# A DoRA forward kernel: block 5 loaded in halves, the resumption moved to the third chunk of block 2, a group of stores moved by two chunks

## The chip, the cores and the metric

One NeuronCore of a Trainium2 chip runs the kernel; the other cores are idle. The metric is the time of one execution on the device in microseconds (us), lower is better. Each kernel was run several times beside the kernel before on the same chip; "faster" and "slower" need more than 2%.

## The reference

```python
W_adapted = W + scale * (lora_A @ lora_B)                       # 256 x 256, rank 16
W_norm    = np.sqrt(np.sum(W_adapted ** 2, axis=0, keepdims=True) + 1e-8)
W_final   = W_adapted / W_norm * m
y = x.reshape(-1, 256) @ W_final                                # x: 16 x 2048 x 256, fp32
```

The weights are small. x has 32768 rows of 1 KB, 33.6 MB, and y is as large: the kernel is a copy through the core with a small matrix product on the way.

## The kernel before

x is cut into 8 blocks of 4096 rows (4 MB), each of 8 chunks of 512 rows; two chunks are a pair, the unit of work. Five block buffers stand in SBUF, and y is written back into the buffer of its x. Blocks 5, 6 and 7 therefore have to wait until blocks 0, 1 and 2 are stored. Loads are issued from SyncE, stores from ScalarE; GpSimd casts a pair to bf16, TensorE transposes it, VectorE copies the transposes to SBUF, TensorE multiplies, ScalarE copies the product back into the x buffer.

```python
loads += [((XBUFS - 1) * CH, CH - 3)]
loads += [(XBUFS * CH - 3 + c, 1) for c in range(3)] + units[XBUFS:]       # (first chunk, chunks)
...
F = NBLK - XBUFS          # 3
G = F * CH                # chunk 24
stores = [(b * CH, CH, 19 + b) for b in range(F - 1)]                      # (first chunk, chunks, issued after chunk)
stores += [(G - CH, CH // 2, 24), (G - CH // 2, CH // 2, 24)]              # stores 2 and 3: block 2
FIRST = len(stores)
stores += [(G + c, 1, G + 3) for c in range(4)]                            # four stores of one chunk
stores += [(G + 4, CH - 4, 47)]                                            # the group: chunks 28-31,
stores += [(b * CH, CH, max(47, (b + 1) * CH - 1)) for b in range(F + 1, NBLK - 1)]  # 32-39, 40-47
stores += [(g0, cnt, g0 + cnt - 1) for g0, cnt in units[-2:]]
HALF = FIRST - 2          # store 2
...
for n in range(len(loads)):                    # SyncE
    if loads[n][0] == XBUFS * CH - 3:
        nc.sync.wait_ge(sem("store0"), 16)
    if loads[n][0] == XBUFS * CH:              # block 5 and all behind it
        for k in range(HALF + 1):
            nc.sync.wait_ge(sem(f"store{k}"), 16)
    if loads[n] == units[-1]:
        nc.sync.wait_ge(sem(f"store{HALF + 1}"), 16)
    load_x(n)
...
for p in range(NPR):                           # GpSimd, one pair at a time
    ...                                        # wait for the load of the pair's chunks
    if p == REST:                              # 15: compute rests until store 2 has landed
        nc.gpsimd.wait_ge(sem(f"store{HALF}"), 16)
    ...                                        # cast
...
with nc.Fori(0, NPR // 2, 1, engines=[PE], head_slot={PE: 128}):   # TensorE
    turned(1)      # transposes of the next pair come before
    product(0)     # the product of this one
    turned(0)
    product(1)
```

Of the kernel before, what the change touches and what calls it, by code (L numbers as in the profile page):

```python
# [11 lines left out]
def kernel(  # L12
# [26 lines left out]
    NBLK = N // BLK  # L39
# [3 lines left out]
    XBUFS = 5  # L43
    CH = DJ // J
# [57 lines left out]
    units = [(b * CH, CH) for b in range(NBLK - 1)]  # L102
    units += [(NCH - CH, CH // 2), (NCH - CH // 2, CH // 2)]
    loads = [(0, 2), (2, 2), (4, CH - 4)] + units[1 : XBUFS - 1]


    loads += [((XBUFS - 1) * CH, CH - 3)]
    loads += [(XBUFS * CH - 3 + c, 1) for c in range(3)] + units[XBUFS:]
    load_of = {g: n for n, (g0, cnt) in enumerate(loads) for g in range(g0, g0 + cnt)}


# [2 lines left out]
    F = NBLK - XBUFS  # L114
    G = F * CH
    stores = [(b * CH, CH, 19 + b) for b in range(F - 1)]
    stores += [(G - CH, CH // 2, 24), (G - CH // 2, CH // 2, 24)]
    FIRST = len(stores)
    stores += [(G + c, 1, G + 3) for c in range(4)]
    stores += [(G + 4, CH - 4, 47)]  # L120
    stores += [(b * CH, CH, max(47, (b + 1) * CH - 1)) for b in range(F + 1, NBLK - 1)]
    stores += [(g0, cnt, g0 + cnt - 1) for g0, cnt in units[-2:]]
    HALF = FIRST - 2

# [4 lines left out]
    def sem(name):  # L129
        if name not in sems:  # L130
            sems[name] = tc.alloc_semaphore(name)
        return sems[name]
# [10 lines left out]
    def load_x(n):  # L143
        nc.sync.dma_start(
            out=in_sbuf(*loads[n]), in_=in_dram(x_flat, *loads[n])
        ).then_inc(sem(f"load{n}"), 16)
# [15 lines left out]
    for n in range(len(loads)):  # L162
        if loads[n][0] == XBUFS * CH - 3:
            nc.sync.wait_ge(sem("store0"), 16)
        if loads[n][0] == XBUFS * CH:


            for k in range(HALF + 1):
                nc.sync.wait_ge(sem(f"store{k}"), 16)
        if loads[n] == units[-1]:  # L170
            nc.sync.wait_ge(sem(f"store{HALF + 1}"), 16)
        load_x(n)

# [12 lines left out]
    for p in range(NPR):  # L186
        b, c = divmod(p, PRB)
# [66 lines left out]
    for g in range(NCH):  # L254
        b, c = divmod(g, CH)
# [123 lines left out]
```

## Time and profile before

| | kernel before |
|---|---|
| time, median of the first 3 runs | 162.56 us (162.53 to 162.67) |
| span of the profiled run | 161.3 us |
| moved | 67.42 MB, mean 418 GB/s |
| both DMA queues' share of the span | 98.1% |
| busiest compute engine | TensorE, 61% |
| last loads end, by packet records | 115.6 to 116.2 us |
| first packets of the group of stores | 115.6 to 116.2 us |

In the profile lines PE is TensorE (PEq its sequencer), POOL GpSimd, DVE VectorE, ACT ScalarE (ACTq issues the stores) and SP SyncE. PEclk is the granted share of TensorE's clock: "warm" below means 1.00, "cold" 0.50. q1 is the queue of the loads, q10 that of the stores; both run on the same 16 DMA engines. A packet's record has its start, duration, size and queue. A DMA share above 1 in a stretch comes from packets that overlap on an engine. The lines on which this reading rests are in the prediction.

### The profile page before, as it was taken

How to read it: one execution, taken by the hardware profiler on the slowest of the kernel's cores; microseconds unless marked ns; L12 is line 12 of the kernel's file. 1: busy time of each engine (PE TensorE's matmuls, PEld its weight loads, DVE VectorE, ACT ScalarE, POOL GpSimd, SP SyncE). 2: the span in 40 equal slices, each digit the busy share in tenths (PEclk: the TensorE clock that was granted, in tenths of full speed). 3: DMA queues.
4: the chain of work that ended last, by engine and by line, in shares of the span. 5: the costliest groups of instructions: out<-in, count | busy, mean ns of one | idle time of the engine just before them, and what ended most of it. 6: DMA issues, size and time to landing. Idle time of an engine off the chain costs nothing. (4 is left out here: it accounts for less than half of the span.)

```text
span 161.3 us, 2012 instructions
## 1 busy us (share of the span) xinstructions
PE 98.1 (61%) x786; PEld 85.6 (53%) x786; DVE 46.6 (29%) x44; ACT 64.1 (40%) x67; POOL 62.9 (39%) x39
## 2 busy tenths in 40 slices
PE   0490899999997920000799949999999980000000
PEld 0260789999996710000689937999799970000000
DVE  0539533535443500000224413445344500000000
ACT  3010068686776370000057643686767681000000
POOL 1174327868684000002938066497667400000000
PEclk9999999999999985555569995999999996555555
DMA  5999999999899999899999999999999999999994
GB/s 163 429 453 459 390 512 398 390 512 398 374 487 439 390 463 456 363 419 422 400 434 424 437 455 422 396 453 431 412 487 398 422 479 398 408 496 398 398 439 211
DMA packets 4357, 67.42 MB, mean 418 GB/s; under 512 B 626, under 2 KB 643, under 8 KB 1667
## 3 DMA queue, kind: packets, MB, share of 16 engines
q1 hardware_dynamic: 2160, 33.82, 49.2%
q10 hardware_dynamic: 2194, 33.59, 48.9%
q14 instruction: 3, 0.02, 0.0%
HBM read 33.85 MB, written 33.55 MB: 418 GB/s over the span
## 5 line engine op out<-in xcount | busy, mean ns | idle before, releaser
L258 ACT COPY x_sb<-y_ps 128x1024 f32<-128x1024 f32 x64 | 62.2, 1015 | 61.5 <-PE y_ps L318 60.2
L199 POOL CAST xb<-x_sb 128x2048 bf16<-128x2048 f32 x32 | 60.4, 1895 | 62.8 <-DMA out_dram<-x_sb 24.7
L318 PE MATMUL y_ps<-w_final,xt 128*128 128x256 bf16 x512 | 66.5, 286 | 2.5 <-PEq L293 2.5
L240 DVE COPY xt<-xt_ps 128x1024 f32<-128x1024 f32 x32 | 39.2, 1224 | 74.3 <-PE xt_ps L304 74.3
L318 PEld LDWEIGHTS y_ps<-w_final,xt 128*128 128x128 bf16 x512 | 52.3, 103 | 10.9 <-issue 3.2
L304 PE MATMUL xt_ps<-identity,xb 128*128 128x128 f32 x264 | 37.2, 288 | 25.7 <-PEq L293 25.7
L304 PEld LDWEIGHTS xt_ps<-identity,xb 128*128 128x128 f32 x264 | 32.3, 150 | 27.7 <-issue 27.2
L274 PE MATMUL y_ps<-identity,a_nat 128*16 128x128 f32 x2 | 0.6, 396 | 4.1 <-DMA a_nat<-in_lora_A_dram 4.1
L285 PE MATMUL y_ps<-sq,ones 128*128 128x256 f32 x4 | 2.1, 675 | 1.6 <-DVE sq L225 1.6
L250 ACT ACTIVATE norm<-y_ps,eps_col 128x256 f32<-128x256 f32 x1 | 0.5, 473 | 5.6 <-PE y_ps L285 5.6
L236 DVE TENSOR_TENSOR w_final<-wam,rnorm 128x256 bf16<-128x256 f32 x2 | 2.5, 1266 | 0.0
L285 PEld LDWEIGHTS y_ps<-sq,ones 128*128 128x128 f32 x4 | 1.2, 326 | 2.3 <-DVE sq L225 2.1
L274 PEld LDWEIGHTS y_ps<-identity,a_nat 128*16 128x16 f32 x2 | 0.1, 88 | 4.1 <-issue 4.1
L248 ACT ACT_TABLE_LOAD x1 | 1.3, 1283 | 2.4 <-issue 2.4
L205 POOL MEMSET xb<- 128x2048 bf16 x1 | 1.8, 1804 | 0.7 <-PE xt_ps L304 0.7
L233 DVE RECIPROCAL rnorm<-norm 128x256 f32<-128x256 f32 x1 | 1.7, 1747 | 0.0
L227 DVE COPY m_all<-y_ps 128x256 f32<-128x256 f32 x1 | 0.4, 424 | 3.3 <-PE y_ps L290 3.3
L290 PE MATMUL y_ps<-m_row,ones 1*128 1x256 f32 x2 | 1.2, 710 | 0.0
L216 DVE CAST b_bf<-b_nat 16x256 bf16<-16x256 f32 x1 | 0.3, 280 | 3.2 <-DMA b_nat<-in_lora_B_dram 3.2
L221 DVE SCALAR_TENSOR_TENSOR wa<-y_ps,w_nat 128x512 f32<-128x512 f32 x1 | 0.7, 692 | 0.8 <-PE y_ps L278 0.8
L278 PE MATMUL y_ps<-b_bf,aT 16*128 16x256 bf16 x2 | 0.6, 402 | 0.5 <-DVE aT L218 0.5
L290 PEld LDWEIGHTS y_ps<-m_row,ones 1*128 1x128 f32 x2 | 0.5, 308 | 0.7 <-issue 0.7
(13 smaller groups left out, 3.3 us busy)
## 6 DMA issues: line engine op xcount, KB each, us to landing
x_sb<-in_x_dram SPq DMA_DIRECT2D x5, 4096.0 KB, 28.7
out_dram<-x_sb ACTq DMA_DIRECT2D x5, 4096.0 KB, 20.9
out_dram<-x_sb ACTq DMA_DIRECT2D x5, 2048.0 KB, 26.7
x_sb<-in_x_dram SPq DMA_DIRECT2D x3, 2048.0 KB, 33.4
x_sb<-in_x_dram SPq DMA_DIRECT2D x1, 2560.0 KB, 44.7
x_sb<-in_x_dram SPq DMA_DIRECT2D x2, 1024.0 KB, 6.0
out_dram<-x_sb ACTq DMA_DIRECT2D x4, 512.0 KB, 43.8
x_sb<-in_x_dram SPq DMA_DIRECT2D x3, 512.0 KB, 19.5
```

The source lines that it names most:

```text
L199: nc.gpsimd.tensor_copy(out=xb_bufs[p % NXB][:], in_=x_bufs[b % XBUFS][:, 2 * c * J : 2 * (c + 1) * J, :],).then_inc(sem("rounded"), 1)
L205: nc.gpsimd.memset(xb_bufs[NPR % NXB][:], 0.0).then_inc(sem("rounded"), 1)
L221: nc.vector.scalar_tensor_tensor(out=wa[:], in0=ab_ps, scalar=float(scale), in1=w_nat[:], op0=ALU.mult, op1=ALU.add).then_inc(dv, 1)
L233: nc.vector.reciprocal(out=rnorm[:], in_=norm[:]).then_inc(dv, 1)
L236: i = nc.vector.tensor_mul(out=w_final[:, t], in0=wam[:, t], in1=rnorm[:])
L240: nc.vector.tensor_copy(out=xt_bufs[p % NXT][:].rearrange("p r t -> p (r t)").bitcast(FP32), in_=xt_ps[p % 2][:],).then_inc(sem("copied"), 1)
L248: nc.scalar.activation(out=warm[:], in_=eps_col[:], func=AF.Sqrt)
L258: nc.scalar.copy(out=x_bufs[b % XBUFS][:, c * J : (c + 1) * J, :], in_=y_ps[g % 2][:]).then_inc(sem("room"), 1)
L285: i = nc.tensor.matmul(n2_ps, ones[:], sq[:, t, :], start=(t == 0), stop=(t == KC - 1))
L290: nc.tensor.matmul(mb_ps, ones[0:1, :], m_row[:], start=True, stop=True).then_inc(pe, 1)
L304: i = nc.tensor.transpose(xt_ps[p % 2][:, j * P : (j + 1) * P], xb_bufs[p % NXB][:, j, :].bitcast(FP32), identity[:],)
L318: i = nc.tensor.matmul(y_ps[h][:, j, :], xt_bufs[p % NXT][:, r : r + P, t], w_final[:, t, :], start=(t == 0 and (j % (J // 2)) == 0), stop ...
```

## The change

Its intent is to resume sooner after the rest (GpSimd's wait for store 2 ahead of pair 15): store 2 covers three chunks instead of four, so that the loads and the compute waiting for it are released earlier, and block 5 comes in two halves, so that its first pairs need not wait for the whole block. The group of three stores is moved from chunk 47 to chunk 49. Since store 3 now begins one chunk earlier, with a chunk whose place the first half of block 7 takes, the wait for it is moved one load earlier too.

```diff
--- before.py
+++ after.py
@@ -105,7 +105,9 @@
 
 
     loads += [((XBUFS - 1) * CH, CH - 3)]
-    loads += [(XBUFS * CH - 3 + c, 1) for c in range(3)] + units[XBUFS:]
+    loads += [(XBUFS * CH - 3 + c, 1) for c in range(3)]
+
+    loads += [(XBUFS * CH, 4), (XBUFS * CH + 4, CH - 4)] + units[XBUFS + 1 :]
     load_of = {g: n for n, (g0, cnt) in enumerate(loads) for g in range(g0, g0 + cnt)}
 
 
@@ -114,11 +116,11 @@
     F = NBLK - XBUFS
     G = F * CH
     stores = [(b * CH, CH, 19 + b) for b in range(F - 1)]
-    stores += [(G - CH, CH // 2, 24), (G - CH // 2, CH // 2, 24)]
+    stores += [(G - CH, 3, 24), (G - CH + 3, CH - 3, 24)]
     FIRST = len(stores)
     stores += [(G + c, 1, G + 3) for c in range(4)]
-    stores += [(G + 4, CH - 4, 47)]
-    stores += [(b * CH, CH, max(47, (b + 1) * CH - 1)) for b in range(F + 1, NBLK - 1)]
+    stores += [(G + 4, CH - 4, 49)]
+    stores += [(b * CH, CH, max(49, (b + 1) * CH - 1)) for b in range(F + 1, NBLK - 1)]
     stores += [(g0, cnt, g0 + cnt - 1) for g0, cnt in units[-2:]]
     HALF = FIRST - 2
 
@@ -167,7 +169,7 @@
 
             for k in range(HALF + 1):
                 nc.sync.wait_ge(sem(f"store{k}"), 16)
-        if loads[n] == units[-1]:
+        if loads[n] == units[-2]:
             nc.sync.wait_ge(sem(f"store{HALF + 1}"), 16)
         load_x(n)
 
```

## The prediction

> **What bounds the kernel now.** I read the page first: the rows of forty slices, the queues, the chain of waits. Lines of the page of the kernel before:
>
> ```profile
> span 161.3 us, 2012 instructions
> ...
> PEclk9999999999999985555569995999999996555555
> DMA  5999999999899999899999999999999999999994
> ...
> q1 hardware_dynamic: 2160, 33.82, 49.2%
> q10 hardware_dynamic: 2194, 33.59, 48.9%
> ...
> PE 10%; ACT 1%; ACTq 1%; issue 0%
> ```
>
> The 16 DMA engines are busy in every slice but the first and the last; loads (q1) and stores (q10) together fill 98.1% of the span. The chain of waits covers only 12% of it: it ends at the issue of the last store, 27 us before the end, since behind that issue lies nothing but a backlog of stores. So only an idle DMA engine can cost time. To see whether any stretch has slack, the view by stretches:
>
> ```profile
> core 0: us, PE busy (x) PEld busy (x) DVE busy (x) ACT busy (x) POOL busy (x), PEclk, DMA share, GB/s
> 4.00:44.00 40.00, 33.64 (x245) 28.39 (x246) 19.62 (x21) 17.85 (x19) 22.74 (x13) 1.00 1.01 435
> ...
> 104.00:113.00 9.00, 9.00 (x85) 8.35 (x83) 4.73 (x4) 6.04 (x7) 6.65 (x4) 1.00 1.03 439
> 113.00:116.00 3.00, 2.71 (x25) 2.23 (x24) 1.39 (x2) 2.05 (x3) 2.20 (x2) 1.00 1.02 429
> 116.00:156.00 40.00, 16.48 (x151) 15.06 (x149) 6.12 (x5) 13.37 (x14) 8.04 (x5) 0.73 1.00 432
> ```
>
> The DMA share (next to last column) is 1.00 or more, also in 113 to 116 us, where the last loads hand over to the last group of stores. 67.42 MB at 432 GB/s take 156.1 us; the other 5.2 us of the span are start, tail and small packets. Order alone cannot win 2% (3.3 us) here; it can lose it.
>
> Last, instructions in order of time around the resumption and the hand-over (start, us, engine, what, idle before it):
>
> ```profile
> 75.73 3.73 POOL L199 CAST xb<-x_sb 128x2048 bf16<-128x2048 f32 x2 [24.69 <-DMA out_dram<-x_sb]
> ...
> 94.03 5.57 POOL L199 CAST xb<-x_sb 128x2048 bf16<-128x2048 f32 x3 [5.21 <-DMA x_sb<-in_x_dram]
> ...
> 96.08 1.11 PE L304 MATMUL xt_ps<-identity,xb 128*128 128x128 f32 x8 [2.32 <-PEq L293]
> ...
> 96.98 3.57 PE L318 MATMUL y_ps<-w_final,xt 128*128 128x256 bf16 x16
> ...
> 104.94 3.73 POOL L199 CAST xb<-x_sb 128x2048 bf16<-128x2048 f32 x2 [1.56 <-DMA x_sb<-in_x_dram]
> ...
> 109.12 1.91 PE L318 MATMUL y_ps<-w_final,xt 128*128 128x256 bf16 x16
> 110.20 1.93 ACT L258 COPY x_sb<-y_ps 128x1024 f32<-128x1024 f32 x2 [0.69 <-PE y_ps L318]
> ...
> 112.23 1.38 ACTq L149 DMA_DIRECT2D out_dram<-x_sb  x3
> ```
>
> GpSimd resumes at 75.73 (chunks 0 to 18 and 19 stored), waits for block 5 until 94.03 and for block 6 until 104.94; chunk 47 is copied out by 112.13, and its store group (10 MB, three DMAs) is issued at 112.23. In the packet records of the trace the loads end at 115.7 to 116.6 and the first packets of that group start at 115.6: no hole, and about 2 us to spare (an issue on an idle ACT queue reached its first packet in 1.5 us at the start of the program: 0.90 to 2.36).
>
> **What the Trainium skill says.** "DMA: Bandwidth & Descriptors", section "Queues, rings and completion order": each DMA engine goes round-robin between the queues that have work, a whole packet at a time. The trace agrees: from 84 to 92 us q1 has 96 packets and q10 95, but 3.15 MB against 0.32. The same page, "Specifications", puts the fabric ceiling at 435 GB/s; the trace holds 432, so the queues are at it. "TensorE: Matmul & The Clock Gate", section "Part 1: The HAM clock gate": after an idle window of some 3.4 us the PE clock is halved, and a busy window restores it; windows run free. The trace agrees and is harsher: the 2.32 us gap before 96.08 was enough, 16 products then took 3.57 instead of 1.91 us, and the granted clock was 0.50 from about 97.0 to 100.4 us.
>
> **The change, part by part.**
>
> Three chunks instead of four. Store 2 has 8 packets an engine; at 432/16 = 27 GB/s a 16 KB packet takes 0.61 us, a 12 KB one 0.46. 8 x 0.15 = 1.2 us earlier resumption: 74.5 instead of 75.73. The bytes only move into the next store (5 chunks), so that both are done as before at about 81; the loads behind the wait queue up behind three small loads on q1 anyway (these run to about 82). Gain in DMA time: none. Compute is 1.2 us earlier, and has slack.
>
> Block 5 in halves. In the packet records block 5's packets begin at 82.3. Each 32 KB load packet (1.21 us) alternates with a 4 KB packet of the four one-chunk stores (0.16): 8 x 1.37 = 11.0 us, which fits 82.3 to 93.2, plus 0.8 for landing = 94.03. In halves the row is 16 KB, so 16 rounds of 0.61 + 0.16 = 12.3 us: the first half is landed at about 82.3 + 6.2 + 0.8 = 89.3, the second at 95.4. So compute on block 5 starts 4.8 us earlier, but 8 more small store packets have been let in, and block 6 lands 8 x 0.16 = 1.3 us later: 106.2 instead of 104.94. The loads' end stays where it was (about 115.9 on the mean engine), as the same bytes have to pass before it.
>
> Compute then. PE needs 2.62 us a pair warm. Pair 20 is cast at 89.3, transposed when PE is free at about 92.5, with no gap; pair 22 is cast 95.4 to 97.3, and the last product PE can do without block 6 (pair 22's, as a product follows the next pair's transposes) ends at about 103.1. Then PE idles until pair 24 is cast: 106.2 + 1.89 = 108.1, a gap of 5.0 us. By what 2.3 us did, the clock falls to half.
>
> Stores at 49 instead of 47. Warm, from the end of pair 24's cast: 0.13 to the transposes, 0.9 to product 23, 2.62 to product 24, 1.08 to the first copy of it, 1.93 for two copies: 6.7 us, so the issue is at 108.1 + 6.7 + 0.1 = 114.9. Cold, the restart at 77.62 (end of the first cast) shows the same steps: its fourth copy ended at 86.99, 9.4 us later, 2.7 more than warm. How long it stays cold depends on where the window falls; I take 1.6 to 3.0 more: issue at 116.5 to 117.9. First packet 1.0 to 1.5 us after that: 117.6 to 119.3. Against loads that end at 115.9 this is a hole of 1.7 to 3.4 us in the DMA queues, the four one-chunk stores being done by then. Nothing fills it later: everything behind it is stores at full rate.
>
> Sum: 162.56 + 0 (earlier resumption) + 0.1 (small packets) + about 2.5 (hole) = 165.1; I put the centre at 164.8 for the cases below.
>
> **The rivals.** (1) PE stays warm, or block 6 lands no later: issue at 114.9 or earlier, first packet at about 116.2, hole 0.3 us or less; time 162.6 to 163.2. For it: the margin between 114.9 and 115.9 is near enough to the start-up time. Against: the clock fell in the smaller gap. (2) The split mends a loss: in 80 to 84 us small packets of both queues meet (by packet records 392 GB/s instead of 432, 0.37 us lost), and a tail; all such losses together are under 1 us: 161.8 to 162.4. For it: PE no longer pauses at 94. Against: that pause cost nothing, as the DMA share was full. (3) The work saved early arrives late at the end: last products later by some 2 to 3 us. Costs nothing: the last store is issued 27 us before the end, over a backlog of 24 us and more. (4) Both the cold phase and the start-up are at their longest, and small packets of the resumed queue add to it: 3.4 us or more, 166 and above.
>
> **Range and chances.** I give the hole of 1.7 to 3.4 us some seven in ten, rivals 1 and 2 together one in four, more than that the rest. Range 162.6 to 166.0. The 2% line lies at 165.8, at the upper end of the hole: slower 0.13, same 0.86, faster 0.01.
>
> **What would show it.** Resumption of GpSimd at about 74.5; casts of block 5 at about 89.3 and 95.4; block 6 at about 106.2; an idle PE of about 5 us before the transposes of pair 24 and a granted clock of 0.50 after it; the issue of three stores after 116; a DMA share well under 1 somewhere in 115 to 119 us; and the same 1.00 in all stretches else. Wrong would be: a group of stores issued before 115 us with a full DMA row (then rival 1), or a time under 162.3 (rival 2: a loss that I took for fixed).

## More of the kernel before

The product of pair p runs after the transposes of pair p + 1. Chunk 47 is in pair 23, so even it needs the cast of pair 24, the first pair of block 6.

## The result

| | before | changed |
|---|---|---|
| median | 162.63 us (162.53 to 163.10, 6 runs) | 164.61 us (163.95 to 165.17, 6 runs) |
| ratio | 1 | 1.0114 (95%: 1.0084 to 1.0144) |
| span of the profiled run | 161.3 us | 163.1 us |

The change costs 1.1%, 2.0 us, which is within 2%. Ratios here are the mean time of one kernel's runs over that of the other's runs of the same rounds, so not quite the ratio of the medians. Executions over 1.5% slower than the fastest of the same kernel are left out of the means.

Lines of the page of the changed kernel, the counterparts of those that the prediction shows:

```profile
span 163.1 us, 2014 instructions
...
PEclk9999999999999965555599999956999999755555
DMA  4999998998999999999999999999499999999996
```

The DMA row, at 8 or 9 in every slice of the kernel before but the first and the last, has a 4 in the 29th, which is 114.2 to 118.3 us. The clock row has a 5 and a 6 in the 27th and 28th, 106.0 to 114.2 us, where the kernel before ran at full clock. The view by stretches of the changed kernel shows the hole with its time:

```profile
core 0: us, PE busy (x) PEld busy (x) DVE busy (x) ACT busy (x) POOL busy (x), PEclk, DMA share, GB/s
112.00:116.00 4.00, 4.00 (x34) 3.53 (x33) 1.23 (x1) 2.74 (x3) 1.78 (x2) 0.87 0.86 369
116.00:118.00 2.00, 2.00 (x21) 1.85 (x20) 1.16 (x1) 1.02 (x2) 1.21 (x2) 1.00 0.12 49
118.00:120.00 2.00, 1.43 (x14) 1.15 (x11) 0.60 (x2) 1.00 (x2) 1.34 (x2) 1.00 1.12 467
```

and the same two first stretches of the kernel before:

```profile
112.00:116.00 4.00, 3.71 (x35) 3.13 (x33) 2.39 (x2) 2.17 (x4) 3.20 (x2) 1.00 1.02 430
116.00:118.00 2.00, 2.00 (x20) 1.88 (x19) 0.33 (x1) 1.81 (x2) 0.85 (x2) 1.00 0.96 410
```

The last two columns are the DMA share and the rate. The share lost is 0.16 of 4 us and 0.84 of 2 us, 2.3 us together. In the packet records the loads end at 115.80 on the mean of the 16 engines and the first stores of the group start at 118.03: 2.2 us. In order of time, the changed kernel came to this so:

```profile
74.68 3.73 POOL L201 CAST xb<-x_sb 128x2048 bf16<-128x2048 f32 x2 [25.09 <-DMA out_dram<-x_sb]
...
89.05 3.89 POOL L201 CAST xb<-x_sb 128x2048 bf16<-128x2048 f32 x2 [1.25 <-DMA x_sb<-in_x_dram]
...
95.16 3.74 POOL L201 CAST xb<-x_sb 128x2048 bf16<-128x2048 f32 x2 [2.22 <-DMA x_sb<-in_x_dram]
...
106.08 3.73 POOL L201 CAST xb<-x_sb 128x2048 bf16<-128x2048 f32 x2 [7.19 <-DMA x_sb<-in_x_dram]
...
108.12 1.94 PE L306 MATMUL xt_ps<-identity,xb 128*128 128x128 f32 x8 [4.92 <-PEq L295]
...
109.86 3.45 PE L320 MATMUL y_ps<-w_final,xt 128*128 128x256 bf16 x16
...
117.13 1.82 ACTq L151 DMA_DIRECT2D out_dram<-x_sb  x3
```

GpSimd resumes 1.05 us sooner than before (75.73), the first half of block 5 is there 4.98 us sooner than the whole block was (94.03), and all that is won so ends in a wait for block 6, which came 1.14 us later than before (104.94). TensorE stood still for 4.92 us; the sixteen products after it took 3.45 us instead of 1.91, and the group of stores was issued 4.90 us later than before (112.23).

### The profile page after: what moved, and what is told of

It is laid out like the page before. It is cut to its first block, busy times and chain, and to the rows that moved or that the text cites. A ratio compares the mean times of both kernels' runs of the same rounds, so it can differ in the third digit from the quotient of the medians.

```text
span 163.1 us, 2014 instructions
## 1 busy us (share of the span) xinstructions
PE 97.9 (60%) x786; PEld 85.6 (52%) x786; DVE 45.0 (28%) x44; ACT 64.1 (39%) x67; POOL 62.8 (39%) x39
## 5 line engine op out<-in xcount | busy, mean ns | idle before, releaser
L320 PE MATMUL y_ps<-w_final,xt 128*128 128x256 bf16 x512 | 65.3, 283 | 2.2 <-PEq L295 2.1
L306 PE MATMUL xt_ps<-identity,xb 128*128 128x128 f32 x264 | 38.1, 292 | 29.4 <-PEq L295 29.4
L306 PEld LDWEIGHTS xt_ps<-identity,xb 128*128 128x128 f32 x264 | 32.8, 151 | 31.6 <-issue 31.2
L232 DVE TENSOR_TENSOR wam<-wa,m_all 128x256 f32<-128x256 f32 x2 | 0.8, 464 | 0.0
```

Of the source, the lines that this page charges most:

```text
L232: i = nc.vector.tensor_mul(out=wam[:, t], in0=wa[:, t], in1=m_all[:])
L306: i = nc.tensor.transpose(xt_ps[p % 2][:, j * P : (j + 1) * P], xb_bufs[p % NXB][:, j, :].bitcast(FP32), identity[:],)
L320: i = nc.tensor.matmul(y_ps[h][:, j, :], xt_bufs[p % NXT][:, r : r + P, t], w_final[:, t, :], start=(t == 0 and (j % (J // 2)) == 0), stop ...
```

## The experiments

The theory: the loss is the hole, and the hole comes from two parts together. The halves let compute run dry ahead of block 6 (a later block 6, a cold TensorE), which takes the margin of the group's issue; chunk 49 takes the rest. The rivals: the halves or the smaller store cost DMA time by themselves; or chunk 49 alone is the loss.

### Which parts: one or two of the three at a time

**a_47**: the changed kernel with the group at chunk 47 again.

```diff
-    stores += [(G + 4, CH - 4, 49)]
-    stores += [(b * CH, CH, max(49, (b + 1) * CH - 1)) for b in range(F + 1, NBLK - 1)]
+    stores += [(G + 4, CH - 4, 47)]
+    stores += [(b * CH, CH, max(47, (b + 1) * CH - 1)) for b in range(F + 1, NBLK - 1)]
```

> The changed kernel with the group of three stores put back from chunk 49 to chunk 47; halves and three chunks stay. My theory (the loss is a hole in the DMA queues because the group is issued too late): the casts, the 5 us PE gap and the clock drop stay as in the changed kernel, but the group is issued 2 chunks earlier, at about 114.5 us (chunk 47's copy ended at 114.36 in the changed trace), its first packets come at about 115.7 to 116, when the loads end, and the hole is 0.3 us or less: 162.6 to 162.9 us. Rival (halves or the three-chunk store cost by themselves: more small packets, more mixing of loads and stores): it stays at 164 or above.

**b_49**: the kernel before with the group at 49 (the same two lines the other way round).

> The kernel before with one part alone, the group of stores at chunk 49 instead of 47. My theory: block 6 lands at 104.9 as before and PE is warm by then, so chunk 49 is copied at about 114.75, the issue is at 114.85, first packets at about 116.0 to 116.3, hole 0.1 to 0.5 us: 162.6 to 163.0 us. So 49 alone is nearly free; it costs only together with the halves. Rival (the later group by itself is the whole loss): 164 or above.

**a_four**: the changed kernel with a store 2 of four chunks.

```diff
-    stores += [(G - CH, 3, 24), (G - CH + 3, CH - 3, 24)]
+    stores += [(G - CH, CH // 2, 24), (G - CH // 2, CH // 2, 24)]
```

> The changed kernel with store 2 of four chunks again (resumption as in the kernel before, at 75.7), halves and 49 kept. My theory: the earlier resumption plays no part, block 6 lands at 106.1 all the same, PE waits for it and goes cold; issue near 117, hole 1.7 to 3.4 us: 164.0 to 165.3, the same as the changed kernel. Rival (the three-chunk store or the earlier resumption is what costs): back to 162.6.

**a_whole**: the changed kernel with block 5 in one load.

```diff
-    loads += [(XBUFS * CH, 4), (XBUFS * CH + 4, CH - 4)] + units[XBUFS + 1 :]
+    loads += units[XBUFS:]
```

> The changed kernel with block 5 in one load again; three chunks and 49 kept. My theory: block 6 lands 1.3 us earlier, at 104.9; PE pauses before block 5 instead (about 3.3 us, half clock for 3.4 to 6 us after it) and catches up by block 6 or is up to 1.3 us late; issue at 114.9 to 116.2, hole 0.1 to 1.5 us: 162.7 to 163.8 us, about 163.2, clearly under the changed kernel. Rival (49 with an earlier resumption is the loss, the halves are innocent): 164.0 or above.

**b_three**: the kernel before with the three-chunk store alone (the pair of lines of a_four the other way round, and the wait for store 3 one load earlier, as in the changed kernel).

> The kernel before with the three-chunk store 2 (and the five-chunk store 3) alone; block 5 whole, group at 47. My theory: GpSimd resumes at about 74.7 instead of 75.7, block 6 lands as before at 104.9, the group is issued at about 112.2 to 113, no hole: 162.5 to 162.9, the same as the kernel before within 0.2 per cent. Rival (an earlier resumption shortens or lengthens the whole): off by over 0.5 us.

| kernel | halves | three chunks | group at | median, us (range, 6 runs) | ratio to before (95%) |
|---|---|---|---|---|---|
| b_three | no | yes | 47 | 162.81 (162.66 to 163.69) | 1.0002 (0.9977 to 1.0028) |
| b_49 | no | no | 49 | 163.15 (162.52 to 164.66) | 1.0015 (0.9978 to 1.0052) |
| a_whole | no | yes | 49 | 163.14 (162.74 to 164.92) | 1.0044 (0.9998 to 1.0090) |
| a_47 | yes | yes | 47 | 163.70 (163.12 to 163.87) | 1.0036 (1.0015 to 1.0058) |
| a_four | yes | no | 49 | 164.81 (163.91 to 165.56) | 1.0108 (1.0073 to 1.0143) |
| changed | yes | yes | 49 | 164.61 (163.95 to 165.17) | 1.0114 (1.0084 to 1.0144) |

The medians come from different rounds: beside b_49, a_whole, a_47 and a_four the kernel before had a median of 163.11 us, beside b_three 162.94, beside the changed kernel 162.63. So the ratios are what can be compared. Three things follow. The three-chunk store plays no part: with it or without it, the loss is 1.1% (a_four against the changed kernel), and alone it does nothing that could be measured (b_three). Halves and 49 each cost about 0.4% or less without the other (the intervals reach to 0.9%), and 1.1% together; neither of the simple rivals stands. And two expectations were missed: a_47 came out at 163.70, where 162.6 to 162.9 was expected, and b_49 at 163.15, where 162.6 to 163.0 was expected, with one run of 164.66. The rounds account for some 0.5 us: for b_49's median, and for over half of a_47's miss. The traces show part of the rest; neither is of the slowest run. Lines in order of time of a_47:

```profile
107.74 3.73 POOL L201 CAST xb<-x_sb 128x2048 bf16<-128x2048 f32 x2 [7.20 <-DMA x_sb<-in_x_dram]
109.78 1.94 PE L306 MATMUL xt_ps<-identity,xb 128*128 128x128 f32 x8 [5.50 <-PEq L295]
...
115.50 3.65 ACTq L151 DMA_DIRECT2D out_dram<-x_sb  x3
```

Here block 6 was there only at 107.74, and the group at 47 was issued at 115.50 instead of the 114.5 expected: a small hole again, 0.2 us by packet records. This was its fastest run; the slower ones left no trace. In b_49 block 6 was not late, and a hole of 1.3 us goes with the clock (its loads ended 0.3 us sooner than those of the kernel before, so not all of it is lost). One stretch of b_49 and, below, the same of a_whole, which both start on block 5 at the same time (96.0 and 96.3) after a gap of over 3 us:

```profile
98.00:102.00 4.00, 4.00 (x21) 3.13 (x20) 1.20 (x1) 1.62 (x2) 1.90 (x1) 0.52 0.99 426
```

```profile
98.00:102.00 4.00, 4.00 (x33) 3.39 (x31) 1.70 (x2) 1.93 (x2) 2.36 (x3) 0.83 1.01 434
```

In b_49 the clock stayed at half until nearly 102 us (granted clock 0.52 in the stretch), in a_whole until 99.4 (0.83), so that TensorE did 33 matmuls in it instead of 21; b_49 issued its group at 115.97, a_whole at 114.91. So in these two traces the issue at chunk 49 follows how long the clock stays at half after the gap, even with block 5 whole. That the two runs of a_whole near 164.9 and the run of b_49 at 164.66 are of this kind was not seen, as only the profiled run leaves a trace.

### The suspected cost once more, and taken away in two ways

**a_51**: the changed kernel with the group at chunk 51 (49 replaced by 51 in both lines).

> The changed kernel with the group at chunk 51 instead of 49: the suspected cost taken once more. PE is warm again by then, so 2.6 us more: issue at about 119.8, first packets at 120.7, hole about 4.9 us: my theory says 167.2 us (166.5 to 167.9). Rival (something else than the hole): under 165.5.

Measured: 167.22 us (166.50 to 168.63), ratio 1.0279 (1.0236 to 1.0323), slower by over 2%. The group was issued at 119.60. Two stretches of a_51:

```profile
116.00:118.00 2.00, 2.00 (x20) 1.84 (x19) 1.23 (x1) 1.31 (x2) 1.21 (x1) 1.00 0.00 0
118.00:120.00 2.00, 2.00 (x21) 1.88 (x20) 0.69 (x1) 1.49 (x2) 1.34 (x2) 1.00 0.00 0
```

Two chunks more made the issue 2.47 us later, the hole 2.4 us longer (4.7 against 2.2, by packet records) and the median 2.6 us longer. Within the noise the added hole is paid for one to one.

**a_early**: the changed kernel, only that the group's first two stores (6 MB, of blocks that were finished long before) are issued at chunk 45, which needs nothing of block 6.

```diff
-    stores += [(G + 4, CH - 4, 49)]
-    stores += [(b * CH, CH, max(49, (b + 1) * CH - 1)) for b in range(F + 1, NBLK - 1)]
+    stores += [(G + 4, CH - 4, 45)]
+    stores += [(b * CH, CH, max(45 if b == F + 1 else 49, (b + 1) * CH - 1)) for b in range(F + 1, NBLK - 1)]
```

> The changed kernel with the first two stores of the group (chunks 28 to 39, 6 MB) issued at chunk 45, which PE reaches before it has to wait for block 6; only the third (block 5) at chunk 49. PE still pauses and goes cold. My theory: these stores are in the queue from about 104.5 us, they mix with the last loads, which end some us later, and no hole is left: 162.4 to 162.9 us. This also shows what the halves cost in DMA time by themselves (estimate 0.1 us). Rival (mixing loads with stores, or the halves, lowers the rate): 163.5 or above.

Measured: 162.94 us (162.62 to 163.71), ratio 1.0016 (0.9990 to 1.0042); the kernel before had 162.94 in the same rounds. TensorE was as cold as ever, but the stores were in the queue. Lines in order of time, then the stretch that was nearly empty in the changed kernel, of a_early:

```profile
104.13 0.89 ACTq L151 DMA_DIRECT2D out_dram<-x_sb  x2
...
108.42 1.94 PE L306 MATMUL xt_ps<-identity,xb 128*128 128x128 f32 x8 [5.49 <-PEq L295]
```

```profile
116.00:118.00 2.00, 2.00 (x21) 1.82 (x20) 1.22 (x1) 1.31 (x2) 1.39 (x1) 1.00 0.98 418
```

The gap in TensorE, 5.49 us, is longer than the 4.92 of the changed kernel, and the loads, mixed with these stores, end at 124.5 us instead of 115.8; neither costs. With the DMA row full, halves and three chunks are free within 0.4%. This is the strongest single piece against the rival that they cost by themselves.

**a_warm**: the changed kernel with work for TensorE in its gap, to see what the clock is worth. The loop is cut at pair 22, and 34 transposes of the identity, whose result nobody reads, stand ahead of the transposes of pair 24.

```diff
+    def fill(p, n):
+        for _ in range(n):
+            nc.tensor.transpose(xt_ps[p % 2][:, 0:P], identity[:], identity[:])
-    with nc.Fori(0, NPR // 2, 1, engines=[PE], head_slot={PE: 128}):
+    with nc.Fori(0, 11, 1, engines=[PE], head_slot={PE: 128}):
...
+    turned(1)
+    product(0)
+    fill(0, 34)
+    turned(0)
+    product(1)
+    with nc.Fori(12, NPR // 2, 1, engines=[PE], head_slot={PE: 128}):
```

> The changed kernel, all of it, with 34 filler transposes of the identity into a free PSUM buffer between the product of pair 22 and the transposes of pair 24 (the loop is cut in two for it), so that PE works through its 5 us gap and keeps the full clock. My theory: clock stays 1.0, the group is issued at about 114.8 us instead of 117.1, first packets 0.9 us later at about 115.7, hole 0 to 0.3 us: 162.5 to 163.0 us. Rival (the late landing of block 6 and the two chunks more are the loss, the clock is a bystander): issue still after 116.5, 164 or above.

Measured: 163.57 us (162.67 to 165.28), ratio 1.0043 (1.0000 to 1.0085); without the run marked slow, 163.30 us (162.67 to 164.85). 162.5 to 163.0 was expected: in part it came so, with a spread that was not expected. So the same kernel was looked at twice more, and once with the group at 47 (**a_warm47**).

> The warm variant at 49 once more, one look, unchanged, to see what its slow samples (164.9 and 165.3 us against 162.7) hold. My theory: with the clock at 1.0 the issue follows the landing of block 6; where the time is above 164, block 6 lands 1 to 2 us later than 106.3 or the clock fell all the same, and the issue is after 116.5; where it is under 163 the issue is near 115. Rival (the slow samples lie elsewhere, in the start or the tail): issue near 115 and a time above 164.

> The same look at the warm variant at 49 a third time, with the same expectations: an issue near 115 us with a time under 163.3 us, or an issue later than 116.5 us with a time above 164 us and a late landing of block 6 or a fallen clock ahead of it. Rival: a time above 164 us with an issue near 115 us.

> The changed kernel with the filler transposes and the group at 47: PE warm, the group two chunks earlier. My theory: issue at about 112.2 us, 3.5 us before the loads end, more margin than any variant with 49; no hole even when one DMA engine lags and block 6 lands 1 to 2 us late: 162.5 to 163.0 us and a narrow spread like that of the kernel before (within 1 us), where the warm variant at 49 spread over 2.6 us. Rival (the spread and the 0.4 per cent left in the variants come from the halves): median 163.5 and the wide spread stay.

Lines in order of time of a_warm (162.92 us in this run), of a_warm_again (164.91 us) and of a_warm_third (163.43 us):

```profile
103.16 3.88 PE L335 MATMUL xt_ps<-identity 128*128 128x128 f32 x34
106.33 5.57 POOL L201 CAST xb<-x_sb 128x2048 bf16<-128x2048 f32 x3 [7.29 <-DMA x_sb<-in_x_dram]
108.37 1.06 PE L306 MATMUL xt_ps<-identity,xb 128*128 128x128 f32 x8 [1.34 <-PEq L295]
...
115.00 3.69 ACTq L151 DMA_DIRECT2D out_dram<-x_sb  x3
```

```profile
107.44 3.73 POOL L201 CAST xb<-x_sb 128x2048 bf16<-128x2048 f32 x2 [8.38 <-DMA x_sb<-in_x_dram]
109.48 1.94 PE L306 MATMUL xt_ps<-identity,xb 128*128 128x128 f32 x8 [2.73 <-PEq L295]
...
117.56 1.81 ACTq L151 DMA_DIRECT2D out_dram<-x_sb  x3
```

```profile
107.41 5.57 POOL L201 CAST xb<-x_sb 128x2048 bf16<-128x2048 f32 x3 [8.25 <-DMA x_sb<-in_x_dram]
109.45 1.06 PE L306 MATMUL xt_ps<-identity,xb 128*128 128x128 f32 x8 [2.84 <-PEq L295]
...
116.08 3.41 ACTq L151 DMA_DIRECT2D out_dram<-x_sb  x3
```

In the first look the clock is full (eight transposes in 1.06 us; the filler, transposes alone from 103.16 to 107.04 us, was enough to hold it at 1.00), the issue is at 115.00 as expected, and no hole is left (the stores' first packets are among the loads' last). In the third the clock is full too, but block 6 is there 1.08 us later and so is the issue: between the two cases that were expected. In the second both go wrong: block 6 is late, the filler ends too soon, a gap of 2.73 us halves the clock (1.94 us for the transposes), and the issue is 2.56 us later than in the first. So the clock makes the issue about 1.5 us later here (117.56 against 116.08 at the same landing), where it was at half for 3.4 us. In the changed kernel it was at half for 6.8 us (106.18 to 113.00), and from the cast of pair 24 to the issue it took 11.05 us against 8.67 in the first and the third look: 2.4 us. That splits the 4.90 us by which the changed kernel's issue is later than the one before: 1.1 from the later block 6, 2.4 from the clock, and 1.4 left for chunk 49 (8.67 against 7.29 us from that cast to the issue in the kernel before, where TensorE was still busy with block 5). This is worked out from single traces. Block 6's landing also varies by 1.1 us on its own. The semaphore records show where: in the second, 15 of the 16 DMA engines had signalled block 6 by 106.29, the last at 107.38. Why one engine lags in some runs stays open.

a_warm47 measured 162.91 us (162.80 to 163.56), ratio 0.9996 (0.9973 to 1.0019), and its spread is 0.8 us. In its trace block 6 came late too (107.37) and the clock fell later, and still the issue was at 114.95, since chunk 47 comes one pair earlier than 49 (2.6 us warm). The expected issue at 112.2 was wrong: even at 47 it waits for block 6.

### More margin than the kernel before has

**b_early**: the kernel before with the first two stores of the group at chunk 45 (as in a_early, 47 for the third).

> The kernel before with the first two stores of the group (6 MB) issued at chunk 45, two chunks before the third: more margin than the kernel before has. My theory: the queues are full already in the kernel before, so nothing is won: 162.5 to 163.1 us, within 0.2 per cent of it. Rival (part of its runs above 163 us have a small hole that more margin closes): median 162.6 or less and no run above 162.9, faster by 0.2 to 0.3 per cent.

Measured: 162.93 us (162.45 to 163.04) against 163.13 (162.49 to 163.81) of the kernel before in the same rounds, ratio 0.9982 (0.9961 to 1.0004): the lowest ratio of all, but not clear of noise, and on what the traces show there is hardly anything to win, since the DMA row is full. That its longest run was 0.8 us shorter (of 6 runs, against 11) hints at the late landings seen above, which would make the kernel before lose a little in some runs; this was not shown.

### All profiled runs in one table

| kernel | group issued at, us | time of that run, us |
|---|---|---|
| a_early | 104.13 | 162.62 |
| b_early | 109.58 | 162.45 |
| b_three | 112.22 | 162.81 |
| before | 112.23 | 162.64 |
| a_whole | 114.91 | 162.74 |
| a_warm47 | 114.95 | 162.80 |
| a_warm | 115.00 | 162.92 |
| a_47 | 115.50 | 163.12 |
| b_49 | 115.97 | 163.26 |
| a_warm_third | 116.08 | 163.43 |
| changed | 117.13 | 164.44 |
| a_four | 117.36 | 164.67 |
| a_warm_again | 117.56 | 164.91 |
| a_51 | 119.60 | 166.77 |

Up to an issue at about 115 us the time does not depend on it (162.45 to 162.92). From 115.97 to 119.60 it rises by 3.51 us in 3.63. Nothing but the time of issue is needed to order these times; runs that were not profiled, the slowest of a_47, a_whole and b_49 among them, are not in it.

## Why the prediction was right

- **The bound.** Only an idle DMA engine could cost time: the variants whose group was well in time (a_early, b_early, b_three, a_warm47) ran within 0.2% of the kernel before, whatever else was done to them, and making the hole 2.4 us longer (a_51) cost 2.6 us.
- **The resumption.** 74.68, predicted 74.5; no effect, as predicted (b_three, a_four).
- **The halves.** Casts at 89.05, 95.16 and 106.08, predicted 89.3, 95.4 and 106.2. The count of rounds between two queues, a small store packet let in for each load packet, gave block 6's delay right (1.14 us, predicted 1.3), and the packet records agree with the mechanism: by 100 us 382 of the 512 small store packets had started, against 265 in the kernel before, 7 more an engine where 8 were predicted.
- **TensorE.** Gap 4.92 us, predicted 5.0; the clock fell. From the end of pair 24's cast (106.08 + 1.89 = 107.97) to the end of chunk 49's copy (117.02) it took 9.05 us, where the warm sum was 6.7 and the cold one up to 9.4.
- **The issue and the hole.** Issue 117.13, predicted 116.5 to 117.9. First packet 0.9 us after it, where 1.0 to 1.5 was taken from the program's start: the one term that was a little too large. Hole 2.2 us, predicted 1.7 to 3.4 (it read the loads' end in the kernel before as 115.7 to 116.6; the data packets end at 115.6 to 116.2, which changes nothing); medians 2.0 us apart; 164.61 us, predicted 164.8.
- **What it did not see.** It took the landing of block 6 as one number. It varies by over 1 us with the slowest DMA engine, so the margin that chunk 49 leaves is not enough even with a warm TensorE, and rival 1, put at 162.6 to 163.2 us, would have had a tail to 164.9 (a_warm's slowest fast run).

## What to carry to other kernels

Where the DMA engines are the bound, ask of each change only whether the DMA engines run out of work, and when (the store queue alone was empty from 108.9 us on in the changed kernel, at no cost while the loads ran): make a table of when the last loads end and when the next stores are issued, and keep a few microseconds of margin (here the issue at 112.23 had some 3 us, as the times rise only after about 115). Work that finishes sooner gains nothing there; here it made TensorE run dry, go cold, and deliver the one thing that the queues needed later. A trigger for stores should hang on the data that is stored (blocks finished long before), not on a later step that waits for a later load.

## What the Trainium skill lacked or had wrong

- "TensorE: Matmul & The Clock Gate", Part 1: it names a full idle window of some 3.4 us (and advises against idle gaps over about that) as what halves the clock. Here gaps of 2.32 us (kernel before) and 2.73 us (a_warm_again) halved it, and one of 2.84 us (a_warm_third) did not. In the clock records of these runs the changes lie whole multiples of 3.41 us apart, so the windows can be placed: the first two gaps put 2.3 us of idle time into one window (93.55 to 96.96 us, 105.64 to 109.05), the third was split into 1.4 and 1.5 over two (border at 107.99). So a window that is partly busy can count as idle, and whether a gap matters depends on where the window falls.
- "DMA: Bandwidth & Descriptors", Specifications: 0.6 us to the first byte for DMAs issued from SyncE or ScalarE. On an idle queue and idle engines it was 0.9 us from the start of the issue to the first packet (117.13 to 118.03, and the same within 0.1 in a_51 and a_four). While the loads still ran it was no longer (114.91 to 115.76, a_whole). In the kernel before it was 3.4 us (112.23 to 115.63): 1.4 us of that passed until the last small packets of the four one-chunk stores, ahead of it in the same queue, had ended (113.61); no run here shows the cause of the rest.
- The same page, on a semaphore that counts 16 engines: it says to wait for all 16 but gives no time for how far they are apart. Here all 16 of block 6 came within 0.6 us in the changed kernel (105.47 to 106.03); in a_warm_again 15 came within 0.7 us and the last 1.1 us later (106.29, 107.38).
